# Feed-forwards of an fp32 trunk: the narrow chunk moved to second place, four chunks in seven block products, two of their weight sums by adding DMAs

## The chip, the cores and the metric

One Trainium2 chip, one of its cores. The time is device microseconds of one execution of the whole program, the median of several runs. A page of the profile and a trace come from one more execution, taken by the hardware profiler.

Engines are named as the profile names them: PE is TensorE (matmuls), DVE is VectorE, ACT is ScalarE, POOL is GpSimd, SP is SyncE, which only issues transfers here. Each takes its instructions from a queue of its own, in order.

## What is computed

A trunk of four layers on 256 tokens of width 1024, in fp32. Each layer is a feed-forward, a token mixer (attention) and a second feed-forward; all eight feed-forwards have the same form:

```python
D_FF = 2816
def swiglu(x, w_in, w_out):
    gate, up = jnp.split(x @ w_in, 2, axis=-1)
    return (jax.nn.silu(gate) * up) @ w_out

for i in range(DEPTH):                       # DEPTH = 4
    g = norm_g[i]
    h = h + 0.5 * rms_norm(swiglu(rms_norm(h, g[0]), ffn_w_in[i, 0], ffn_w_out[i, 0]), g[1])
    m = rms_norm(h, g[2])
    ...                                      # one of three kinds of attention
    h = h + rms_norm(m, g[3])
    h = h + 0.5 * rms_norm(swiglu(rms_norm(h, g[4]), ffn_w_in[i, 1], ffn_w_out[i, 1]), g[5])
```

The attention layers are not touched by the change.

## The kernel before

**Precision.** Every fp32 operand of a matmul is split in two float32r parts: ACT casts (`hi`, line 156), DVE subtracts (`lo`, line 157). A product takes three matmuls for each k-tile of 128: hi by hi, lo by hi, hi by lo. The 256 tokens are two token tiles, t = 0 and 1.

**Chunks.** `ffn` (line 283) walks over the 2816 columns of gate and up in six chunks: five of 512 and, last, one of 256. Each chunk computes gate and up for its columns, forms g = silu(gate) * up, transposes g on PE (`turn`, line 425, into `tpg`, then split to `gh` and `gl`) and adds g times its rows of w_out to the banks `y` (`out`, line 436). The w_out part of a chunk follows one chunk later, in units of two k-tiles: two units for a full chunk (k = 0 and 2), one for the narrow one.

**Two forms of a chunk.** `plain` (line 443) multiplies each of gate and up with both token tiles, eight block products of four k-tiles (12 matmuls each) for a full chunk. `wino` (line 466) takes the four quarters of the weights, b00, b01 (gate and up of the first 512 rows), b10, b11 (of the other 512), and makes seven products of sums, in the manner of Winograd and Strassen: b00, b10, t2, t1, t3, b11, t4, in this order, with the first w_out unit of the chunk before behind t2 and the second behind b11. B, A and C are the PSUM banks `pb`, `pa` and `pc`; b00 goes to B alone, ACT copies the bank (line 483, `sl<-pb`), and then t2, t1 and b11 add to the same bank, with a copy by ACT between them. `WINO` names the chunks in this form: 2 and 4.

**Sums of weights.** `plan_wino` (line 358) makes four DVE sums of 128x2048 for a chunk (line 373): b00 += b01, b01 += b11, t2 = b00 + b11, later t2 += b10.

**Buffers and order.** Loads are 1 MB transfers on SP into `raw` buffers, nine of them (`RAWS`). A split unit (hi and lo of 128x2048) lives in one of four buffers (`UNITS`); `fill` (line 398) prepares the next unit of the list as soon as fewer than four are alive. So the split of the fourth unit ahead can start when PE has read the one before it for the last time. The order of each engine's queue is fixed when the program is built, by a scheduler that goes by its own costs. After the last chunk come the rest of the w_out products, `end` (the norm and the new x, in `finish`, line 210) for each token tile, and `turn_x`, which transposes x for the next phase.

Of the kernel before, what the change touches and what calls it, by code (L numbers as in the profile page):

```python
# [16 lines left out]
P = 128  # L17
# [19 lines left out]

RAWS = 9
UNITS = 4
WINO = (2, 4)  # L40

IN_NAMES = ["x", "norm_g", "ffn_w_in", "ffn_w_out", "diff_w_in", "diff_w_out", "diff_lambda",
            "diff_subln", "moba_w_in", "moba_w_out", "nsa_w_in", "nsa_w_out", "nsa_cmp_pe",
# [3 lines left out]
class Trunk:  # L47
# [235 lines left out]
    def ffn(self, l, f, X, ahead, end):  # L283
        nc = self.nc
        with self.tc.tile_pool(name=f"ffn{l}{f}", bufs=2, reuse_waits="tile") as pool:
            w_in, w_out = self.a["ffn_w_in"][l, f], self.a["ffn_w_out"][l, f]
            chunks = [(c, min(512, D_FF - c)) for c in range(0, D_FF, 512)]
            last = len(chunks) - 1
            y = [None, None]
            G, U = {}, {}  # L290
# [32 lines left out]
            def split(n, of, done=False):  # L323
                live["unit"] += 1
                self.n += 1
                nk, w, m = shape.get(of, (4, 512, 4))
                hi = self.wt.tile([P, nk, w], F32R, tag="hi", name=f"hi{self.n}")
                lo = self.wt.tile([P, nk, w], F32R, tag="lo", name=f"lo{self.n}")
                v = R[of][:, :nk * w].rearrange("p (k n) -> p k n", n=w)
                for k in range(0, nk, m):  # L330
                    self.hilo(v[:, k:k + m], hi[:, k:k + m], lo[:, k:k + m])
                if done:
                    free(of)
                U[n] = hi, lo, nk, w

            def close(n):
                U.pop(n)
                live["unit"] -= 1
# [5 lines left out]
            def plan_plain(j):  # L344
                c0, w = chunks[j]
                for b, o in (("g", 0), ("u", D_FF)):
                    if w == 512:
                        for h in range(2):
                            plan((j, b, h), (w_in, h * 512, 4, o + c0, w))
                    else:  # L350
                        plan((j, b, 0), (w_in, 0, 8, o + c0, w))

            def plan_out(j):
                c0, w = chunks[j]
                for k in range(0, w // P, 2):
                    plan((j, "o", k), (w_out, c0 + k * P, 2, 0, D))

            def plan_wino(j):


                c0, w = chunks[j]
                name = lambda n: (j, n)
                quarter = lambda k, u: (w_in, k * 512, 4, u * D_FF + c0, w)
                ko = [(j - 1, "o", k) for k in (0, 2)]
                c1 = chunks[j - 1][0]
                osrc = [(w_out, c1 + k * P, 2, 0, D) for k in (0, 2)]
                for n, src in ((name("b00"), quarter(0, 0)), (name("b01"), quarter(0, 1)),
                               (name("b10"), quarter(1, 0)), (name("b11"), quarter(1, 1)), (name("t2"), None),
                               (ko[0], osrc[0]), (ko[1], osrc[1])):
                    loads.append(lambda n=n, src=src: raw(n, src))  # L370

                def add(to, a, b):
                    nc.vector.tensor_tensor(R[name(to)], R[name(a)], R[name(b)], op=ALU.add)  # L373

                def quarters(n, then=()):
                    split(name(n), name(n))
                    for x in then:
                        add(*x)

                def last_of(n, of, before=None, gone=None):  # L380
                    if before:
                        add(*before)
                    if gone:
                        free(name(gone))
                    split(name(n), name(of), True)

                preps.extend([
                    lambda: quarters("b00", [("b00", "b00", "b01")]),
                    lambda: quarters("b10", [("b01", "b01", "b11"), ("t2", "b00", "b11")]),
                    lambda: split(name("t2"), name("t2")),  # L390
                    lambda: split(ko[0], ko[0], True),
                    lambda: last_of("t1", "b00"),
                    lambda: last_of("t3", "b01"),
                    lambda: last_of("b11", "b11"),
                    lambda: split(ko[1], ko[1], True),
                    lambda: last_of("t4", "t2", ("t2", "t2", "b10"), "b10")])

            def fill():
                while loads and live["raw"] < RAWS:
# [25 lines left out]
            def turn(j, t):  # L425
                n = chunks[j][1] // P
                g = G.pop((j, t))
                tp = self.tp.tile([P, 4, P], F32, tag="mm", name=f"tpg{l}{f}_{j}_{t}")
                for k in range(n):
                    nc.tensor.transpose(tp[:, k, :], g[:, k * P:(k + 1) * P], self.ident)  # L430
                gh = self.gt.tile([P, 4, P], F32R, tag="gh", name=f"gh{l}{f}_{j}_{t}")
                gl = self.gt.tile([P, 4, P], F32R, tag="gl", name=f"gl{l}{f}_{j}_{t}")
                self.hilo(tp[:, :n], gh[:, :n], gl[:, :n])
                G[j, t] = (gh, gl)
# [31 lines left out]
            def wino(j):  # L466
                def times(ps, x, at, n, first):
                    self.product(ps, x, [(at, unit((j, n)))], first, True, more=True)
                    close((j, n))

                def o(t, k):
                    out(j - 1, t, (k,))
                    if t == 1:
                        close((j - 1, "o", k))
                    fill()

                tile = lambda tag, t: pool.tile([P, 512], F32, tag=tag, name=f"{tag}{l}{f}_{j}_{t}")
                add = lambda d, x: nc.vector.tensor_tensor(d, x, d, op=ALU.add)
                s24, s31 = SUMS
                B = bank("pb")  # L480
                times(B, X[0][0], 0, "b00", True)
                sl0 = tile("sl", 0)
                nc.scalar.copy(sl0, B)
                fill()
                turn(j - 1, 0)
                A = bank("pa")
                times(A, X[0][0], 4, "b10", True)
                add(sl0, A)
                nc.scalar.activation(sl0, sl0, AF.Silu, scale=X[0][1])
                fill()  # L490
                turn(j - 1, 1)
                times(B, s24, 0, "t2", False)
                sl1 = tile("sl", 1)
                nc.scalar.copy(sl1, B)
                fill()
                o(0, 0)
                o(1, 0)
                times(B, s31, 4, "t1", False)
                g1 = tile("g", 1)
                nc.scalar.copy(g1, B)  # L500
                fill()
                C = bank("pc")
                times(C, s31, 0, "t3", True)
                add(g1, C)
                fill()
                times(B, s24, 4, "b11", False)
                up(0, B, 512, sl0, j, nr[0])
                fill()
                o(0, 2)
                o(1, 2)  # L510
                times(C, X[1][0], 4, "t4", False)
                add(sl1, C)
                nc.scalar.activation(sl1, sl1, AF.Silu, scale=X[1][1])
                up(1, g1, 512, sl1, j, nr[1], g1)
                fill()
                del G[j - 1, 0], G[j - 1, 1]

            plan_plain(0)
            for j in range(1, last):
                if j in WINO:  # L520
                    plan_wino(j)
                else:
                    plan_plain(j)
                    plan_out(j - 1)
            plan_plain(last)
            plan_out(last - 1)
            plan_out(last)

            SUMS, nr = [], []
# [7 lines left out]

            plain(0, [(0, 0), (1, 0), (0, 1), (1, 1)], [lambda: None, lambda: None, early])
            zig = [(0, 0), (0, 1), (1, 0), (1, 1)]
            for j in range(1, last):  # L540
                if j in WINO:
                    wino(j)
                    continue
                plain(j, zig, [lambda: turn(j - 1, 0), lambda: turn(j - 1, 1)])
                for t in range(NT):
                    out(j - 1, t, (0, 2))
                for k in (0, 2):
                    close((j - 1, "o", k))
                fill()
                del G[j - 1, 0], G[j - 1, 1]  # L550
            plain(last, zig, [lambda: turn(last - 1, 0), lambda: turn(last - 1, 1)])
            out(last - 1, 0, (0, 2))
            turn(last, 0)
            turn(last, 1)
            ahead()
            out(last, 0, (0,))
            turn_x = end(0, y[0])
            out(last - 1, 1, (0, 2))
            for k in (0, 2):
                close((last - 1, "o", k))  # L560
            turn_x()
            out(last, 1, (0,))
            self.later_x = end(1, y[1])

    def turn_x(self):
# [757 lines left out]
```

## Time and profile before

| | |
|---|---|
| median of three runs | 1990.72 us (1990.71 to 1993.12) |
| the profiled execution | 1993.53 us, of it the span 1991.8 us |
| PE, matmul | 1962.8 us busy, 99% of the span, 9904 matmuls |
| DVE | 1481.6 us, 74% |
| ACT | 1153.8 us, 58% |
| POOL | 127.6 us, 6% |
| mean granted TensorE clock | 0.998 of full speed |
| DMA, all 16 engines | 361.51 MB on SP's queue, 52% of their time |

The span runs from the first to the last instruction of the profiled execution; its own time has 1.7 us around that. Matmuls overlap, so their pace is read from starts and not from durations. A share of busy time is a mean over stages that have different limits. The feed-forward that is read most below is the second one, from about 320 to 500 us.

### The profile page before, as it was taken

How to read it: one execution, taken by the hardware profiler on the slowest of the kernel's cores; microseconds unless marked ns; L12 is line 12 of the kernel's file. 1: busy time of each engine (PE TensorE's matmuls, PEld its weight loads, DVE VectorE, ACT ScalarE, POOL GpSimd, SP SyncE). 2: the span in 40 equal slices, each digit the busy share in tenths (PEclk: the TensorE clock that was granted, in tenths of full speed). 3: DMA queues.
4: the chain of work that ended last, by engine and by line, in shares of the span. 5: the costliest groups of instructions: out<-in, count | busy, mean ns of one | idle time of the engine just before them, and what ended most of it. 6: DMA issues, size and time to landing. Idle time of an engine off the chain costs nothing.

```text
span 1991.8 us, 25602 instructions
## 1 busy us (share of the span) xinstructions
PE 1962.8 (99%) x9904; PEld 1625.0 (82%) x9904; DVE 1481.6 (74%) x1944; ACT 1153.8 (58%) x1625; POOL 127.6 (6%) x239
## 2 busy tenths in 40 slices
PE   7999999999999999999999999999999999999998
PEld 6888878888888878888888888678888888878887
DVE  6877677877778666778777777877777877677875
ACT  6555566555555566565554665865466556566553
POOL 0000210000000120000000032000000000210000
PEclk9999999999999999999999999999999999999999
DMA  9543638445664356564646374164538543638540
GB/s 365 209 148 127 207 120 313 170 144 202 230 232 148 106 190 217 185 232 148 222 156 214 129 191 157 64 234 147 211 130 313 192 144 116 206 107 306 191 146 23
DMA packets 168650, 363.14 MB, mean 182 GB/s; under 512 B 7760, under 2 KB 36688, under 8 KB 168528
## 3 DMA queue, kind: packets, MB, share of 16 engines
q1 hardware_dynamic: 168528, 361.51, 52.0%
q8 instruction: 78, 1.28, 0.3%
q14 instruction: 44, 0.36, 0.1%
HBM read 360.43 MB, written 1.05 MB: 181 GB/s over the span
## 4 chain that ended last, share of the span: by engine, by line
PE 92%; DVE 3%; ACT 2%; issue 1%; POOL 0%; DMA 0%; SPq 0%; DVEq 0%; POOLq 0%; ACTq 0%
PE ps L152 31%; PE y L244 9%; PE y L246 9%; PE y L245 9%; PE pb L152 9%; PE pc L152 4%; PE pw L667 4%; PE pw L669 4%; PE pw L668 4%; PE pa L152 2%; PE tpg L430 2%; DVE lo L157 1%; PE sc L741 1%; PE tpx L181 1%; ACT e L752 1%
## 5 line engine op out<-in xcount | busy, mean ns | idle before, releaser
L157 DVE TENSOR_TENSOR lo<-raw,hi 128x2048 fp32r<-128x2048 f32 (+3 forms) x486 | 876.3, 1821 | 313.4 <-ACT hi L156 309.6
L156 ACT CAST hi<-raw 128x2048 fp32r<-128x2048 f32 (+3 forms) x486 | 733.6, 1528 | 508.2 <-PE ps L152 167.3
L152 PE MATMUL ps<-hi,xh 128*128 128x512 f32 (+1 forms) x1024 | 377.7, 369 | 1.8 <-ACT xh L156 1.2
L152 PE MATMUL ps<-hi,xl 128*128 128x512 f32 (+1 forms) x1024 | 372.7, 364 | 0.0
L152 PE MATMUL ps<-lo,xh 128*128 128x512 f32 (+1 forms) x1024 | 372.4, 364 | 0.2 <-DVE lo L157 0.2
L244 PE MATMUL y<-hi,gh 128*128 128x512 f32 x704 | 276.2, 392 | 0.0
L245 PE MATMUL y<-lo,gh 128*128 128x512 f32 x704 | 274.3, 390 | 0.0
L246 PE MATMUL y<-hi,gl 128*128 128x512 f32 x704 | 271.2, 391 | 0.0
L152 PEld LDWEIGHTS ps<-hi,xh 128*128 128x128 f32 x1024 | 193.9, 189 | 31.8 <-ACT xh L156 2.1
L152 PEld LDWEIGHTS ps<-hi,xl 128*128 128x128 f32 x1024 | 193.6, 189 | 31.6 <-DVE xl L157 1.1
L152 PEld LDWEIGHTS ps<-lo,xh 128*128 128x128 f32 x1024 | 194.0, 189 | 30.3 <-DVE lo L157 1.1
L667 PE MATMUL pw<-hi,xh 128*128 128x512 f32 (+2 forms) x432 | 165.3, 383 | 0.0
L246 PEld LDWEIGHTS y<-hi,gl 128*128 128x128 f32 x704 | 131.5, 188 | 32.1 <-DVE gl L157 4.3
L669 PE MATMUL pw<-hi,xl 128*128 128x512 f32 (+2 forms) x432 | 156.4, 362 | 0.0
L668 PE MATMUL pw<-lo,xh 128*128 128x512 f32 (+2 forms) x432 | 156.2, 362 | 0.0
L244 PEld LDWEIGHTS y<-hi,gh 128*128 128x128 f32 x704 | 132.2, 188 | 28.1 <-ACT gh L156 1.7
L245 PEld LDWEIGHTS y<-lo,gh 128*128 128x128 f32 x704 | 132.3, 188 | 26.0
L373 DVE TENSOR_TENSOR raw<-raw,raw 128x2048 f32<-128x2048 f32 x64 | 145.0, 2286 | 0.0
L119 POOL TENSOR_TENSOR st<-st,negh 128x1 f32<-128x1 f32 (+1 forms) x56 | 45.1, 806 | 1491.6 <-DVE st L206 1395.5
L667 PEld LDWEIGHTS pw<-hi,xh 128*128 128x128 f32 x432 | 82.0, 190 | 18.3 <-issue 8.2
L752 ACT ACTIVATE e<-e,st 128x128 f32<-128x128 f32 (+1 forms) x160 | 71.7, 450 | 40.6 <-DVE st L749 39.8
L157 DVE TENSOR_TENSOR gl<-tpg,gh 128x512 fp32r<-128x512 f32 (+1 forms) x96 | 61.0, 642 | 45.6 <-ACT gh L156 45.6
(212 smaller groups left out, 2648.6 us busy)
## 6 DMA issues: line engine op xcount, KB each, us to landing
raw<-in_ffn_w_in SPq DMA_DIRECT2D x172, 1024.0 KB, 7.0
raw<-in_ffn_w_out SPq DMA_DIRECT2D x88, 1024.0 KB, 5.6
raw<-in_diff_w_in SPq DMA_DIRECT2D x24, 1024.0 KB, 5.2
raw<-in_moba_w_in SPq DMA_DIRECT2D x12, 1024.0 KB, 5.3
raw<-in_nsa_w_in SPq DMA_DIRECT2D x9, 1024.0 KB, 5.1
raw<-in_diff_w_out SPq DMA_DIRECT2D x8, 1024.0 KB, 4.9
gpre<-in_norm_g SPq DMA_DIRECT2D x12, 512.0 KB, 5.9
gpost<-in_norm_g SPq DMA_DIRECT2D x12, 512.0 KB, 7.4
```

Source lines behind the costliest of these rows:

```text
L119: self.nc.gpsimd.tensor_tensor(r, v, src, op=ALU.pow)
L152: nc.tensor.matmul(out, l, r, start=first and i == 0, stop=last and i == len(steps) - 1, skip_group_check=more)
L156: self.nc.scalar.copy(hi, src)
L157: self.nc.vector.tensor_tensor(lo, src, hi.bitcast(F32), op=ALU.subtract)
L244: nc.tensor.matmul(y[b], x[0][:, kt, :], hi[:, k, s], start=f, stop=False)
L245: nc.tensor.matmul(y[b], x[0][:, kt, :], lo[:, k, s], start=False, stop=False)
L246: nc.tensor.matmul(y[b], x[1][:, kt, :], hi[:, k, s], start=False, stop=l)
L373: nc.vector.tensor_tensor(R[name(to)], R[name(a)], R[name(b)], op=ALU.add)
L667: nc.tensor.matmul(out, x[0][:, kt, :], hi[:, k, :], start=first and i == 0, stop=False)
L668: nc.tensor.matmul(out, x[0][:, kt, :], lo[:, k, :], start=False, stop=False)
L669: nc.tensor.matmul(out, x[1][:, kt, :], hi[:, k, :], start=False, stop=last and i == len(todo) - 1)
L752: nc.scalar.activation(e[:, c, :], e[:, c, :], AF.Exp, scale=-1.0, bias=top[:, c:c + 1], accum_out=tot[:, c:c + 1])
```

## The change

`WINO` becomes (2, 3, 4, 5). The narrow chunk moves from the end to second place, index 1. So chunk 0 is plain and full, chunk 1 plain and narrow, and chunks 2 to 5 are full chunks in seven products. Of the four big sums in each of them, two stay on DVE (b00 += b01 and t2 = b00 + b11); the two others (b01 += b11 and t2 += b10) are transfers issued by POOL that add to what lies in the destination. The order of sums and splits in the list of units is set anew for it. In the last chunk the second w_out unit of the chunk before comes behind t4, and the products after the last chunk are put in another order. A setting of the build, `dynamic_dma_scratch_size`, goes from 1024 to 2048.

```diff
-WINO = (2, 4)
+WINO = (2, 3, 4, 5)
...
-            chunks = [(c, min(512, D_FF - c)) for c in range(0, D_FF, 512)]
+            chunks = [(c, 512) for c in range(0, D_FF - 256, 512)]
+            chunks.insert(1, (D_FF - 256, 256))
...
-                ko = [(j - 1, "o", k) for k in (0, 2)]
-                c1 = chunks[j - 1][0]
-                osrc = [(w_out, c1 + k * P, 2, 0, D) for k in (0, 2)]
+                c1, w1 = chunks[j - 1]
+                ko = [((j - 1, "o", k), (w_out, c1 + k * P, 2, 0, D)) for k in range(0, w1 // P, 2)]
...
+                def add_by_dma(to, b):
+                    nc.gpsimd.dma_start(R[name(to)], R[name(b)], accum_op=ALU.add)
 
                 def quarters(n, then=()):
                     split(name(n), name(n))
                     for x in then:
-                        add(*x)
-
-                def last_of(n, of, before=None, gone=None):
-                    if before:
-                        add(*before)
+                        (add if len(x) == 3 else add_by_dma)(*x)
+
+                def last_of(n, of, gone=None):
+                    split(name(n), name(of), True)
                     if gone:
                         free(name(gone))
-                    split(name(n), name(of), True)
-
+
+                outs = [lambda n=n: split(n, n, True) for n, _ in ko]
                 preps.extend([
                     lambda: quarters("b00", [("b00", "b00", "b01")]),
-                    lambda: quarters("b10", [("b01", "b01", "b11"), ("t2", "b00", "b11")]),
-                    lambda: split(name("t2"), name("t2")),
-                    lambda: split(ko[0], ko[0], True),
+                    lambda: quarters("b10", [("t2", "b00", "b11"), ("b01", "b11")]),
+                    lambda: quarters("t2", [("t2", "b10")]),
+                    outs[0],
                     lambda: last_of("t1", "b00"),
                     lambda: last_of("t3", "b01"),
-                    lambda: last_of("b11", "b11"),
-                    lambda: split(ko[1], ko[1], True),
-                    lambda: last_of("t4", "t2", ("t2", "t2", "b10"), "b10")])
+                    lambda: last_of("b11", "b11")])
+                if j < last:
+                    preps.extend(outs[1:])
+                preps.append(lambda: last_of("t4", "t2", "b10"))
+                if j == last:
+                    preps.extend(outs[1:])
...
-                o(0, 2)
-                o(1, 2)
+                if j < last and chunks[j - 1][1] == 512:
+                    o(0, 2)
+                    o(1, 2)
...
-            plain(last, zig, [lambda: turn(last - 1, 0), lambda: turn(last - 1, 1)])
-            out(last - 1, 0, (0, 2))
             turn(last, 0)
+            out(last - 1, 0, (2,))
+            ahead()
+            out(last, 0, (0, 2))
             turn(last, 1)
-            ahead()
-            out(last, 0, (0,))
             turn_x = end(0, y[0])
-            out(last - 1, 1, (0, 2))
-            for k in (0, 2):
-                close((last - 1, "o", k))
+            out(last - 1, 1, (2,))
+            close((last - 1, "o", 2))
+            out(last, 1, (0,))
             turn_x()
-            out(last, 1, (0,))
+            out(last, 1, (2,))
```

DVE's queue in the second feed-forward, from the split of b11 in chunk 2 on (`raw387_2965` is its b11, `raw389_2971` its t2; the splits of `raw400_3094` and `raw402_3100` and the next are units of chunk 3, which is plain), before:

```order
L157 TENSOR_TENSOR lo418_3313<-raw387_2965,hi418_3312 128x2048
L373 TENSOR_TENSOR raw389_2971<-raw389_2971,raw380_2861 128x2048
L157 TENSOR_TENSOR lo420_3343<-raw396_3025,hi420_3342 128x2048
L157 TENSOR_TENSOR lo422_3364<-raw389_2971,hi422_3363 128x2048
L478 TENSOR_TENSOR g01_2_1_3360<-pc425_3371,g01_2_1_3360 128x512
L157 TENSOR_TENSOR lo426_3386<-raw400_3094,hi426_3385 128x2048
L422 SCALAR_TENSOR_TENSOR g01_2_0_3403<-pb412_3238,st390_2984,sl01_2_0_3251 128x512
L157 TENSOR_TENSOR lo428_3406<-raw402_3100,hi428_3405 128x2048
L157 TENSOR_TENSOR lo430_3435<-raw411_3236,hi430_3434 128x2048
L478 TENSOR_TENSOR sl01_2_1_3310<-pc425_3371,sl01_2_1_3310 128x512
```

and now DVE's queue from the split of b11 in chunk 3 to t2 of chunk 4 (`raw413_3245` is b11 and `raw416_3266` t2 of chunk 3; `raw421_3320` the second w_out unit; `raw423_3350`, `raw424_3352`, `raw430_3431` and `raw433_3452` are b00, b01, b10 and b11 of chunk 4, `raw436_3482` its t2):

```order
L157 TENSOR_TENSOR lo437_3507<-raw413_3245,hi437_3506 128x2048
L157 TENSOR_TENSOR lo439_3537<-raw421_3320,hi439_3536 128x2048
L482 TENSOR_TENSOR g01_3_1_3554<-pc444_3564,g01_3_1_3554 128x512
L157 TENSOR_TENSOR lo441_3557<-raw416_3266,hi441_3556 128x2048
L157 TENSOR_TENSOR lo445_3579<-raw423_3350,hi445_3578 128x2048
L426 SCALAR_TENSOR_TENSOR g01_3_0_3595<-pb431_3433,st396_3004,sl01_3_0_3446 128x512
L372 TENSOR_TENSOR raw423_3350<-raw423_3350,raw424_3352 128x2048
L157 TENSOR_TENSOR lo446_3598<-raw430_3431,hi446_3597 128x2048
L372 TENSOR_TENSOR raw436_3482<-raw423_3350,raw433_3452 128x2048
L482 TENSOR_TENSOR sl01_3_1_3504<-pc444_3564,sl01_3_1_3504 128x512
L157 TENSOR_TENSOR lo447_3628<-raw436_3482,hi447_3627 128x2048
L426 SCALAR_TENSOR_TENSOR g01_3_1_3554<-g01_3_1_3554,st397_3006,sl01_3_1_3504 128x512
```

The sum of t2 with b10 has left the queue, and the two sums of the next chunk stand between the splits of b00, b10 and t2, ahead of the small sum for `sl` of token tile 1.

ACT's queue at the start of chunk 2 in the second feed-forward (`raw389_2971` is t2, `raw394_3019` the first w_out unit, `pb412` the bank of b00), before:

```order
L156 CAST hi409_3228<-raw389_2971 128x2048
L156 CAST hi410_3232<-raw394_3019 128x2048
L483 COPY sl01_2_0_3251<-pb412_3238 128x512
L156 CAST hi413_3253<-raw376_2845 128x2048
L156 CAST gh01_1_0_3264<-tpg01_1_0_3259 128x512
```

and now at the start of chunk 4 (`raw436_3482` is t2, `raw438_3510` the first w_out unit, `pb450` the bank of b00, `raw423_3350` t1 and `raw424_3352` t3):

```order
L156 CAST hi447_3627<-raw436_3482 128x2048
L518 ACTIVATE sl01_3_1_3504<-sl01_3_1_3504,st368_2826 128x512
L156 CAST hi448_3647<-raw438_3510 128x2048
L487 COPY sl01_4_0_3666<-pb450_3653 128x512
L156 CAST hi451_3668<-raw423_3350 128x2048
L156 CAST gh01_3_0_3679<-tpg01_3_0_3674 128x512
L156 CAST hi454_3698<-raw424_3352 128x2048
L156 CAST gh01_3_1_3708<-tpg01_3_1_3703 128x512
```

The Silu of the chunk before now stands between the cast of t2 and the copy of b00's bank.

## Rows read from the trace of the kernel before

**Rows 1.** The page's first part: busy us, share of the span and count by engine.
```profile
PE 1962.8 (99%) x9904; PEld 1625.0 (82%) x9904; DVE 1481.6 (74%) x1944; ACT 1153.8 (58%) x1625; POOL 127.6 (6%) x239
```

**Rows 2.** PE's waits over the whole span, longest in total first.
```profile
engine line waited for: us in total, times, longest us
PE tpx L181 <- DVE xg L173: 8.2, 1, 8.2
PE tpf L698 <- DVE on L969: 4.0, 4, 1.2
...
PE ps L152 <- ACT xh L156: 1.2, 1, 1.2
```

**Rows 3.** PE's instructions in order: start us, duration us, engine, line, operation.
```profile
167.77 0.28 PE L152 MATMUL ps<-hi,xl 128*128 128x256 f32 x1
167.89 0.28 PE L152 MATMUL ps<-hi,xh 128*128 128x256 f32 x1
...
371.03 0.39 PE L152 MATMUL pb<-hi,xh 128*128 128x512 f32 x1
371.25 0.39 PE L152 MATMUL pb<-lo,xh 128*128 128x512 f32 x1
...
377.29 0.47 PE L152 MATMUL pb<-hi,sh 128*128 128x512 f32 x1
...
388.37 0.39 PE L152 MATMUL pc<-hi,sh 128*128 128x512 f32 x1
```

**Rows 4.** Busy time of each engine in a block-product chunk and in a feed-forward.
```profile
core 0: us, PE busy (x) PEld busy (x) DVE busy (x) ACT busy (x) POOL busy (x), PEclk, DMA share, GB/s
371.02:401.95 30.93, 30.93 (x141) 25.42 (x140) 26.12 (x17) 21.83 (x16) 0.00 (x0) 1.00 0.76 273
323.00:490.00 167.00, 167.00 (x807) 139.76 (x806) 124.98 (x93) 89.59 (x80) 1.08 (x2) 1.00 0.52 186
```

**Rows 5.** DVE's instructions around chunk 2 of the second feed-forward, columns as in 3.
```profile
366.84 4.49 DVE L373 TENSOR_TENSOR raw<-raw,raw 128x2048 f32<-128x2048 f32 x2
373.38 6.70 DVE L157 TENSOR_TENSOR lo<-raw,hi 128x2048 fp32r<-128x2048 f32 x3 [2.05 <-ACT hi L156]
379.99 0.69 DVE L157 TENSOR_TENSOR gl<-tpg,gh 128x512 fp32r<-128x512 f32 x1
...
393.20 0.68 DVE L478 TENSOR_TENSOR g<-pc,g 128x512 f32<-128x512 f32 x1
393.80 2.28 DVE L157 TENSOR_TENSOR lo<-raw,hi 128x2048 fp32r<-128x2048 f32 x1
396.00 0.74 DVE L422 SCALAR_TENSOR_TENSOR g<-pb,st,sl 128x512 f32<-128x512 f32 x1
396.66 2.28 DVE L157 TENSOR_TENSOR lo<-raw,hi 128x2048 fp32r<-128x2048 f32 x1
```

**Rows 6.** ACT's instructions in the same feed-forward, columns as in 3.
```profile
332.27 0.69 ACT L416 ACTIVATE sl<-ps,st 128x512 f32<-128x512 f32 x1
332.86 1.90 ACT L156 CAST hi<-raw 128x2048 fp32r<-128x2048 f32 x1
...
371.44 3.71 ACT L156 CAST hi<-raw 128x2048 fp32r<-128x2048 f32 x2 [9.18 <-DVE raw L373]
375.06 0.57 ACT L483 COPY sl<-pb 128x512 f32<-128x512 f32 x1
375.53 1.91 ACT L156 CAST hi<-raw 128x2048 fp32r<-128x2048 f32 x1
377.35 0.58 ACT L156 CAST gh<-tpg 128x512 fp32r<-128x512 f32 x1
377.82 1.92 ACT L156 CAST hi<-raw 128x2048 fp32r<-128x2048 f32 x1
...
388.57 0.59 ACT L500 COPY g<-pb 128x512 f32<-128x512 f32 x1 [0.31 <-PE pb L152]
```

**Rows 7.** DMA issues: tensor, queue, count, KB each, median us to landing.
```profile
raw<-in_ffn_w_in SPq DMA_DIRECT2D x172, 1024.0 KB, 7.0
...
out<-h SPq DMA_DIRECT2D x4, 256.0 KB, 2.0
```

More of the change, by code (lines that the diff above doesn't have):

```diff
@@ L363, in plan_wino @@
                 quarter = lambda k, u: (w_in, k * 512, 4, u * D_FF + c0, w)
-                ko = [(j - 1, "o", k) for k in (0, 2)]
-                c1 = chunks[j - 1][0]
-                osrc = [(w_out, c1 + k * P, 2, 0, D) for k in (0, 2)]
+                c1, w1 = chunks[j - 1]
+                ko = [((j - 1, "o", k), (w_out, c1 + k * P, 2, 0, D)) for k in range(0, w1 // P, 2)]
                 for n, src in ((name("b00"), quarter(0, 0)), (name("b01"), quarter(0, 1)),
-                               (name("b10"), quarter(1, 0)), (name("b11"), quarter(1, 1)), (name("t2"), None),
-                               (ko[0], osrc[0]), (ko[1], osrc[1])):
+                               (name("b10"), quarter(1, 0)), (name("b11"), quarter(1, 1)), (name("t2"), None), *ko):
                     loads.append(lambda n=n, src=src: raw(n, src))
@@ L515, in wino @@
                 fill()
-                del G[j - 1, 0], G[j - 1, 1]
+                if j < last:
+                    del G[j - 1, 0], G[j - 1, 1]
             plan_plain(0)
-            for j in range(1, last):
+            for j in range(1, last + 1):
                 if j in WINO:
@@ L524, in ffn @@
                     plan_out(j - 1)
-            plan_plain(last)
-            plan_out(last - 1)
             plan_out(last)
@@ L539, in ffn @@
             zig = [(0, 0), (0, 1), (1, 0), (1, 1)]
-            for j in range(1, last):
+            for j in range(1, last + 1):
                 if j in WINO:
@@ L1311 @@
     nc = bacc.Bacc("TRN2", target_bir_lowering=False, num_devices=1,
-                   dynamic_dma_scratch_size=1024)
+                   dynamic_dma_scratch_size=2048)
     arrays, args = {}, {}
```

## Prediction

> **What bounds the kernel now.** I read the page first, then PE's list of waits, then one block-product chunk of the second feed-forward. PE is busy for 99% of the span [rows 1] and its list of waits [rows 2] is all but empty: the largest entry is the start, 8.2 us, the next ones belong to attention (tpf, sc, tph: 4.0 us or less in all), the first products of a phase (ps) follow with 1.2, and no bank of a block-product chunk (pa, pb, pc) stands in it. So the bound is PE's count of instructions. The pace is read from starts, since the durations overlap: a 512-column matmul every 0.227 us (371.03 to 371.25), a 256-column one every 0.12 us [rows 3]. A plain full chunk has 96 input matmuls, a block-product chunk 7 x 12 = 84. The granted clock is 1.00 in all windows read [rows 4].
>
> The second thing to see is how near the next engine is. In the chunk from 371.02 to 401.95 us PE works 30.93 us, DVE 26.12 and ACT 21.83 [rows 4]. That chunk follows a plain one and is followed by a plain one, which take DVE fewer splits, and PE never waits. The question is what four such chunks in a row do.
>
> **The removed work.** Two more chunks of each of eight feed-forwards use seven products: 2 x 8 x 12 = 192 matmuls fewer, 192 x 0.2267 = **43.5 us** less PE time. The narrow chunk and the products with w_out keep their counts and only move.
>
> **The added work.** A split is an ACT cast and a DVE subtraction; from one start to the next they take 1.81 and 2.20 us (371.44 and 375.06; 373.38 and 379.99) [rows 5, 6]. A block-product chunk needs seven splits instead of four, so DVE gets 2 x 3 x 2.2 = 13.2 us more in each feed-forward. Its big sums stay at eight: two in each of four chunks, instead of four in two, the other two by DMA. In a run of such chunks DVE has in each 9 splits, 2 sums (11 x 2.2), two gl (1.2), three small sums (1.8) and two products with the gate (1.3): 28.5 us against PE's 30.9. On average it fits. The chain does not, as the queues' order shows.
>
> **The chain of a third or fourth block chunk.** Let 0 be the start of its b00 product. PE before it: t4 from -2.72, the second w_out unit from -8.16, b11 from -10.88, t3 from -13.60. The first w_out unit ends five matmuls before t3, at -14.7. Only four split units may live, so the split of the second one starts then: ACT sees PE's end 0.2 us later (388.37 to 388.57) [rows 3, 6], casts for 1.91, and DVE begins at -12.6. From there DVE works through its queue without a hole: lo 2.2, small sum 0.6, lo of t4 2.2, lo of b00 2.2, gate product 0.66, sum b00+b01 2.2, lo of b10 2.2, and the sum for t2, which ends at +1.95. ACT's queue then has, in this order, the cast for t2 (1.81, from 2.05), a Silu (0.6, by 332.27 to 332.86), the cast of a w_out unit (1.81) and the copy of b00's bank (0.57) [rows 6]. The copy ends near 6.9. PE may not add t2 into that bank sooner, and it got there at 2.72 + 0.36 (transposes) + 2.8 = 5.9: **it waits 1.1 us**. In the chunk of before this sum ends at 371.33, 0.3 after b00's start (371.03), the copy at 375.63, and t2 starts at 377.29: 1.7 us to spare [rows 3, 5, 6].
>
> A second wait follows in the same chunk. Behind the copy ACT casts t1, gh of token tile 0, t3, and then gh of tile 1: 0.47 for the copy, 1.81, 0.47, 1.81 and 0.58 for the last [rows 6], from the copy's start at 6.3 to 11.4, some 4.6 us after t2's start. PE wants it one product, one turn and four matmuls after that, at 4.0: **0.6 us** more. Round the loop, from one t2 to the next, this makes 32.4 us for 30.9, 1.5 lost.
>
> **The second block chunk** comes behind the first, which has one w_out unit instead of two, since the narrow chunk has two k-tiles: PE has 5.44 us less to do while DVE saves only 2.2. From t1's end (-8.16): +0.2, a copy 0.47, the cast of b00 1.91, so DVE's lo of b00 runs from -5.5; then 2.2 + 0.6 + 2.2 + 2.2 + 2.2 and a gate product of 0.75, done at +4.6. PE's transposes of that very g stand behind b00, at 2.72: 1.95 us late. The copy, as above, ends at 8.9 and t2 could start at 7.85: 1.1 more. Together **3.1 us**.
>
> **The first** follows the narrow chunk: PE has 12.2 us of products and 10.9 of w_out there while DVE has four splits; its t2 sum ends some 4 us before b00 starts. Nothing lost. **The end** of a feed-forward: the chain from the last y to the transposed x has five DVE steps, now with one gl (0.6) among them; PE has 22 matmuls (5.0 us) before it needs x, as before, and now a turn (0.36) too. Before it had no wait there [rows 2]. I take 0; were the cover gone it would be under 1 us at each of seven ends between a feed-forward and what follows it.
>
> Sum for one feed-forward: 3.1 + 1.5 + 1.5 + 0.6 (the second wait of the last chunk) = 6.7 us, eight times 53.6 us.
>
> **The adding DMAs.** Two in each block chunk, 64 in all, on POOL's queue, which has 1.08 us of work in the 167 us of a feed-forward [rows 4]; behind them stand only the pow of the norm at its end. The first (b01 += b11) starts when DVE has read b01, at -2.45 in the chain above, and ACT's cast of t3 wants it at 9.1: a window of 11.5 us. The second (t2 += b10) has 13.9. No row shows such a transfer. Below, a small store lands in 2.0 us; above, three loads one after the other, 3 x 7.0 = 21 [rows 7]. Loads ran at 273 GB/s with a DMA share of 0.76 [rows 4], so 1 MB fills all engines for 2.9 us, and a load's landing has 4.1 on top. An add reads two megabytes; I take 2 x 2.9 + 4.1 = 9.9 us, nearest to a load, inside both windows: nothing. Each microsecond past a window holds ACT's queue, with the gh cast and the next chunk's casts behind it, and costs 3 x 8 = 24 us; at 21 it would be over 200. DVE is not slowed by fewer sums; a gain beyond the sums already taken from its queue is excluded.
>
> The Trainium skill ("DMA: Bandwidth & Descriptors", section on the anatomy of one DMA, SWDGE path) gives a GpSimd transfer about 2.0 us plus its bytes at 436 GB/s; by that, an estimate, such an add takes 4.4 us and the windows are wide. The rows for loads here (7.0) are slower than that. The same page ("Issuing engines are not separate DMA queues") says that transfers from all queues share the same 16 engines, which speaks against the change; no run here shows it yet.
>
> **The sum.** The profiled execution took 1993.53 us (span 1991.8), 2.8 above the median of 1990.72. 1993.5 - 43.5 + 53.6 = 2003.6, less 2.8: **2001 us**.
>
> **The rivals.**
> 1. The waits do not bite, faster: 1990.7 - 43.5 = 1947 with none of them, 1972 if only the second chunk's 3.1 us are paid (24.8). For it: the loop is 32.4 us of which I need only 1.5 less, 5%, and every hand-over is read to 0.1 us at best; PE shows no such wait today [rows 2]. Against: the steps are back to back in fixed queues, with durations that repeat to 1%.
> 2. The DMA engines become the bound, slower still. Six loads fill them 17.5 us of a chunk's 32.4, which leaves 7.4 for each add. If an add costs three passes (read, read, write), 8.8 us, the chunk takes 35.1: 2.7 x 3 x 8 = 65 us more, 2066. It decides from 7.4 us of engine time or 11.5 us to landing. For it: share 0.76 in today's chunk [rows 4]. Against: the mean over a feed-forward is 0.52.
> 3. The waits and the gain cancel: 6.7 comes out as 5.4, 1991. That the products are not removed is no rival: PE's queue is shorter by just 192.
>
> **How the numbers follow.** Forecast (1995 to 2015) 0.46; rival 2 or late adds (2015 and up) 0.23; rival 3, within 0.2% (which is about what a measurement of this kernel can tell from no change) 0.12; rival 1 0.19, of it 0.06 below 1972. So slower 0.69, same 0.12, faster 0.19. The range goes from 1972 to 2066; about 0.06 lies below and 0.10 above. The forecast's own range is 1995 to 2015.
>
> **What would show it.** PE busy near 1920 us and a list of waits that is no longer empty: tpg and pb on ACT's sl copy or DVE's g, about 2.0 us once and 1.1 us three times in each feed-forward, y on ACT's gh, 0.6 us. DVE idle shrinks in chunks three to five. Adds that land within 11 us, with no ACT cast waiting for a DMA, would confirm the cover. It is wrong if PE's waits sum to far less than 50 us, or if casts wait for the adds.

## The result, and the profile after

The changed kernel takes **2005.25 us** (median of 4 runs, 2003.10 to 2006.29) against 1991.90 of the kernel before on the same chip: ratio 1.0065, 95% interval 1.0052 to 1.0077. It is slower, by about what was forecast (2001 us, 1995 to 2015). The profiled execution took 2004.23 us with a span of 2002.3, which is 10.5 more than before, at the same mean granted clock (0.998). Since 43.5 us of products are gone, 54.0 us of PE's time went into something new (by the medians 13.4 + 43.5 = 56.9).

The page of the changed kernel, its busy times (1), the queue of the adding transfers (3: packets, MB, share of the engines), chain (4) and two of its DMA issues (6):

```profile
span 2002.3 us, 25733 instructions
PE 1932.5 (97%) x9712; PEld 1584.9 (79%) x9712; DVE 1609.4 (80%) x2040; ACT 1257.2 (63%) x1721; POOL 188.6 (9%) x303
q0 software_dynamic: 9216, 67.11, 17.6%
PE 79%; ACT 8%; DVE 7%; issue 3%; POOL 0%; ACTq 0%; DVEq 0%; POOLq 0%
...
raw<-in_ffn_w_in SPq DMA_DIRECT2D x172, 1024.0 KB, 8.4
raw<-raw POOLq DMA_DIRECT2D x64, 1024.0 KB, 7.0
```

PE has 192 instructions fewer than in [rows 1], and is now 97% busy instead of 99%. In the chain that ended last PE has 79%, where it had 92% before; ACT and DVE have grown from 5% to 15%. PE's list of waits (engine and line, tile, what it waited for: us in total, times, longest), which was empty of block chunks in [rows 2]:

```profile
PE pb L152 <- ACT sl L487: 21.1, 24, 0.9
PE tpg L434 <- DVE g L426: 14.1, 8, 1.8
...
PE y L244 <- ACT gh L156: 5.1, 24, 0.2
```

All three are new, with just the counts of the forecast: the copy of b00's bank 24 times (three block chunks in each of eight feed-forwards), g 8 times (the second block chunk), gh 24 times. They add up to 40.3 us. A recorded wait begins at the modelled end of the matmul before it, 0.39 us behind its start, while the next one would have started 0.227 behind it; so each wait is 0.17 us longer than recorded, and 56 of them make 9.5 us more. Together that is 49.8 of the 54.0; the remaining 4.2 are not placed.

PE in the second feed-forward of the changed kernel, at the three kinds of wait (start, duration, ..., idle before and what ended it):

```profile
389.40 0.39 PE L152 MATMUL pb<-hi,xl 128*128 128x512 f32 x1
391.55 0.66 PE L434 MATMUL tpg<-ident,g 128*128 128x128 f32 x4 [1.76 <-DVE g L426]
394.59 0.39 PE L152 MATMUL pa<-hi,xl 128*128 128x512 f32 x1
395.80 0.50 PE L152 MATMUL pb<-hi,sh 128*128 128x512 f32 x1 [0.83 <-ACT sl L487]
400.38 0.50 PE L244 MATMUL y<-hi,gh 128*128 128x512 f32 x1 [0.21 <-ACT gh L156]
424.10 0.60 PE L434 MATMUL tpg<-ident,g 128*128 128x128 f32 x4
428.34 0.51 PE L152 MATMUL pb<-hi,sh 128*128 128x512 f32 x1 [0.90 <-ACT sl L487]
456.68 0.60 PE L434 MATMUL tpg<-ident,g 128*128 128x128 f32 x4
```

The first transposes of a chunk (tpg) mark its loop: 391.55 to 424.10 is 32.55 us, 424.10 to 456.68 is 32.58, for 30.93 in [rows 4]. And the chain that PE waits for, DVE's part and ACT's, in the third block chunk (b00 starts at 421.37):

```profile
421.10 2.28 DVE L372 TENSOR_TENSOR raw<-raw,raw 128x2048 f32<-128x2048 f32 x1
...
425.42 2.29 DVE L157 TENSOR_TENSOR lo<-raw,hi 128x2048 fp32r<-128x2048 f32 x1 [1.44 <-ACT hi L156]
```

```profile
423.49 1.90 ACT L156 CAST hi<-raw 128x2048 fp32r<-128x2048 f32 x1 [8.16 <-DVE raw L372]
425.30 0.72 ACT L518 ACTIVATE sl<-sl,st 128x512 f32<-128x512 f32 x1
425.92 1.89 ACT L156 CAST hi<-raw 128x2048 fp32r<-128x2048 f32 x1
427.71 0.57 ACT L487 COPY sl<-pb 128x512 f32<-128x512 f32 x1
```

ACT sits idle for 8.16 us until DVE's sum for t2 ends at 423.4, then does cast, Silu, the cast of the w_out unit and the copy in a row; PE starts t2 as the copy ends. In [rows 3, 5] the same sum ended 0.3 us behind b00's start, here 2.0.

### The profile page after: what moved, and what is told of

The parts are those of the page before. It is cut to its first block, busy times and chain, and to the rows that moved or that the text cites. A ratio compares the mean times of both kernels' runs of the same rounds, so it can differ in the third digit from the quotient of the medians.

```text
span 2002.3 us, 25733 instructions
## 1 busy us (share of the span) xinstructions
PE 1932.5 (97%) x9712; PEld 1584.9 (79%) x9712; DVE 1609.4 (80%) x2040; ACT 1257.2 (63%) x1721; POOL 188.6 (9%) x303
## 3 DMA queue, kind: packets, MB, share of 16 engines
q0 software_dynamic: 9216, 67.11, 17.6%
## 4 chain that ended last, share of the span: by engine, by line
PE 79%; ACT 8%; DVE 7%; issue 3%; POOL 0%; ACTq 0%; DVEq 0%; POOLq 0%
PE ps L152 13%; PE pb L152 12%; PE y L246 9%; PE y L244 9%; PE y L245 9%; PE pc L152 6%; ACT hi L156 5%; PE pa L152 4%; PE pw L670 4%; PE pw L672 4%; PE pw L671 3%; DVE lo L157 3%; DVE raw L372 2%; PE tpg L434 1%; ACT gh L156 1%
## 5 line engine op out<-in xcount | busy, mean ns | idle before, releaser
L157 DVE TENSOR_TENSOR lo<-raw,hi 128x2048 fp32r<-128x2048 f32 (+3 forms) x534 | 984.7, 1861 | 251.3 <-ACT hi L156 250.8
L156 ACT CAST hi<-raw 128x2048 fp32r<-128x2048 f32 (+3 forms) x534 | 824.8, 1563 | 481.6 <-DVE raw L372 189.9
L152 PE MATMUL ps<-hi,xh 128*128 128x256 f32 (+1 forms) x512 | 175.4, 342 | 1.9 <-ACT xh L156 1.3
L152 PE MATMUL pb<-hi,sh 128*128 128x512 f32 x384 | 153.1, 399 | 21.1 <-ACT sl L487 21.1
L152 PE MATMUL ps<-lo,xh 128*128 128x256 f32 (+1 forms) x512 | 173.2, 338 | 0.2 <-DVE lo L157 0.2
L152 PE MATMUL ps<-hi,xl 128*128 128x256 f32 (+1 forms) x512 | 172.9, 338 | 0.0
L152 PE MATMUL pb<-lo,sh 128*128 128x512 f32 x384 | 151.8, 395 | 0.0
L152 PE MATMUL pb<-hi,sl 128*128 128x512 f32 x384 | 149.5, 389 | 0.0
L152 PEld LDWEIGHTS ps<-hi,xh 128*128 128x128 f32 x512 | 97.6, 191 | 13.2 <-ACT xh L156 2.2
L152 PEld LDWEIGHTS ps<-lo,xh 128*128 128x128 f32 x512 | 97.6, 191 | 11.2 <-DVE lo L157 1.1
```

Of the source, the lines that this page charges most:

```text
L152: nc.tensor.matmul(out, l, r, start=first and i == 0, stop=last and i == len(steps) - 1, skip_group_check=more)
L156: self.nc.scalar.copy(hi, src)
L157: self.nc.vector.tensor_tensor(lo, src, hi.bitcast(F32), op=ALU.subtract)
```

## The experiments

Theory A is the forecast's: latency of that one chain through fixed queues, with the adding transfers hidden. B: the transfers cost the time. C: DVE or ACT has too much to do in block chunks. All were timed beside the kernel before, whose medians lie between 1990.89 and 1991.44 us there, and the ratios are to it. Edits are to the changed kernel where nothing else is said; the kernels of the first two experiments and of the second one under "The w_out unit ahead of t2" leave sums out and so compute something else.

### One DVE sum less

```diff
-                    lambda: quarters("b00", [("b00", "b00", "b01")]),
+                    lambda: quarters("b00"),
```

> The changed kernel without one of the two sums that DVE makes in each block-product chunk (b00 += b01 is left out; 32 sums of 2.2 us in all). Theory A, the prediction's chain (the sum for t2 ends 1.95 us behind the start of b00, ACT's copy of the bank stands behind it): all of the chain comes 2.2 us earlier, so the copy (late by 1.1), the transposes of the second block chunk (late by 1.95) and the gh cast (late by 0.6) are in time but for some 0.8 us once a feed-forward. PE's waits on the copy and on g fall from 35.2 us recorded to under 8, the loop of a third or fourth block chunk from 32.6 to 30.9 us, the time from 2005 to 1950 to 1965. Theory B, the adding transfers fill the DMA engines or hold up casts: they are all still there, time 1998 to 2006.

Measured: 1954.99 us, ratio 0.9814 (0.9798 to 0.9830). PE's waits on the copy, on gh and on g are gone from its list; the new entry, and two starts a loop apart:

```profile
PE pb L152 <- DVE lo L157: 4.8, 8, 1.2
...
415.95 0.60 PE L434 MATMUL tpg<-ident,g 128*128 128x128 f32 x4
446.85 0.60 PE L434 MATMUL tpg<-ident,g 128*128 128x128 f32 x4
```

The loop is 30.90 us, and the span (1953.5) is 5.2 above 1991.8 - 43.5 = 1948.3. So the products are saved in full, and 2.2 us of one chain decide over 50 us. B falls: all 64 transfers are still there. So are the moved narrow chunk, the new end and the larger `dynamic_dma_scratch_size`, which leaves them some 5 us at most. C is not excluded by this run, since DVE has less to do.

### No adding transfers

```diff
-                    lambda: quarters("b10", [("t2", "b00", "b11"), ("b01", "b11")]),
-                    lambda: quarters("t2", [("t2", "b10")]),
+                    lambda: quarters("b10", [("t2", "b00", "b11")]),
+                    lambda: quarters("t2"),
```

> The changed kernel without its 64 adding transfers (b01 += b11 and t2 += b10 are left out). Theory A, the transfers land in their windows and cost nothing: 2002 to 2007, the same waits of PE on ACT's copy and on g as in the changed kernel (35.2 us recorded). Theory B, their 5.5 us of all DMA engines each slow the loads, or a cast waits for them: faster by 10 us or more, to 1995 or below. What DVE does is unchanged.

Measured: 2004.30 us, ratio 1.0063 (1.0048 to 1.0078), as with them. The waits are the same to 0.1 us:

```profile
PE pb L152 <- ACT sl L487: 21.0, 24, 0.9
PE tpg L434 <- DVE g L426: 14.0, 8, 1.8
```

So the transfers are hidden, and B is out.

### The two sums back on DVE

```diff
-                    lambda: quarters("b10", [("t2", "b00", "b11"), ("b01", "b11")]),
-                    lambda: quarters("t2", [("t2", "b10")]),
+                    lambda: quarters("b10", [("t2", "b00", "b11"), ("b01", "b01", "b11")]),
+                    lambda: quarters("t2", [("t2", "t2", "b10")]),
```

> The changed kernel with its two adding transfers made by DVE instead (b01 += b11 behind the sum for t2, t2 += b10 behind the difference of t2). DVE gets 2 x 2.2 us more in each block chunk, 32.9 us of work in a loop that takes 32.6. Theory A, with the adds hidden in the changed kernel: the loop grows by 2 to 4.4 us, the time to 2050 to 2120. Theory B (the transfers cost about what the sums would): 1995 to 2015.

Measured: 2040.13 us, ratio 1.0239 (1.0224 to 1.0254): slower by 34.9 us than with the transfers, short of the 45 that were the least expected. PE waits 29.3 us for g (14.1 with the transfers), and the loop, read at the last two of these starts, is 33.56 us, 1.0 more instead of 2 to 4.4:

```profile
PE tpg L434 <- DVE g L426: 29.3, 9, 4.0
...
398.98 1.11 PE L434 MATMUL tpg<-ident,g 128*128 128x128 f32 x4 [3.96 <-DVE g L426]
431.65 0.60 PE L434 MATMUL tpg<-ident,g 128*128 128x128 f32 x4
465.21 0.60 PE L434 MATMUL tpg<-ident,g 128*128 128x128 f32 x4
```

Two sums of 2.2 us more make a loop 1.0 longer: part of them goes into gaps that DVE has while it waits for ACT (1.44 us at 425.42 above is one). DVE is now busy for 33.12 of the 33.56 us. So the transfers do save time against sums on DVE, by less than theory A said and by more than B. Part of the 34.9 us is the clock, which no theory had: in or just behind each of seven waits for g of about 4.0 us the granted clock falls to the lower of its two levels (1.2 of 2.4 GHz) for a while, as at 398.98, where four transposes take 1.11 us instead of 0.60. The mean granted clock is 0.991 instead of 0.998, by an estimate from these two figures up to some 14 us of PE's time in 2038.7.

### The copy first

Same instructions, other queues. `issue_after(x)` puts what its block issues behind x in the queue of x's engine; besides, the split of the first w_out unit is issued no longer at the end of the chunk before, and `unit` fills only if its unit is missing.

```diff
-                nc.scalar.copy(sl0, B)
-                fill()
-                turn(j - 1, 0)
+                cp = nc.scalar.copy(sl0, B).ins
+                with self.tc.issue_after(cp):
+                    ga, gd = turn(j - 1, 0)
+                with self.tc.issue_after(ga), self.tc.issue_after(gd):
+                    if live["unit"] < UNITS:
+                        preps.pop(0)()
...
-                fill()
-                turn(j - 1, 1)
                 times(B, s24, 0, "t2", False)
+                ga, gd = turn(j - 1, 1)
+                with self.tc.issue_after(ga), self.tc.issue_after(gd):
+                    fill()
```

> The changed kernel, same instructions, other order of the queues in a block-product chunk: ACT copies b00's bank before it casts the w_out unit, gh of token tile 0 comes right behind the copy, gh of tile 1 (whose transposes now come behind t2) ahead of the casts of t1 and t3. Theory A (the latency of one chain through fixed queues): in the third and fourth block chunk the copy ends near 4.5 us behind b00's start where PE wants it at 5.9, so the loop falls to 30.9 to 31.3 us; the transposes of the second block chunk, which wait for g, are still 1.9 us late. 1965 to 1985. Theory C (DVE or ACT have too much work in a row of block chunks, whatever the order): the loop stays at 32.0 to 32.6, the time at 1998 to 2006. Theory B (DMA): 1998 to 2006 as well.

Measured: 1978.45 us, ratio 0.9936 (0.9921 to 0.9950), faster than both. ACT in the third block chunk, PE's waits, and the loop:

```profile
418.81 1.91 ACT L156 CAST hi<-raw 128x2048 fp32r<-128x2048 f32 x1 [8.36 <-DVE raw L372]
...
421.24 0.56 ACT L489 COPY sl<-pb 128x512 f32<-128x512 f32 x1
421.70 0.59 ACT L156 CAST gh<-tpg 128x512 fp32r<-128x512 f32 x1
...
PE tpg L435 <- DVE g L427: 14.1, 8, 1.8
PE pb L152 <- DVE lo L157: 5.1, 16, 0.4
...
419.22 0.60 PE L435 MATMUL tpg<-ident,g 128*128 128x128 f32 x4
450.72 0.60 PE L435 MATMUL tpg<-ident,g 128*128 128x128 f32 x4
```

With not an instruction less, the wait on the copy is gone (21.1 us before) and the one on gh too, and the loop is 31.50, a little over the 30.9 to 31.3 expected. That rules C out as the cause of 32.6. The order of several things changed together here, so the gain isn't split between the copy and the other moves. The wait for g in the second block chunk is untouched, to the tenth.

### The w_out unit ahead of t2

```diff
+                o(0, 0)
+                o(1, 0)
                 times(B, s24, 0, "t2", False)
                 sl1 = tile("sl", 1)
                 nc.scalar.copy(sl1, B)
                 fill()
-                o(0, 0)
-                o(1, 0)
```

with the split of t2, and DVE's sum for it, behind that unit's split in `preps`, and the order inside the chunk held by `issue_after`.

> The changed kernel, same instructions, with the first w_out unit of the chunk before placed ahead of the product t2 instead of behind it, on PE and in the list of splits; the DVE sum for t2 comes behind that unit's split, the g product of tile 1 ahead of the small sum of the next chunk. PE then wants t2 at 11.6 us behind b00's start instead of 6.2, which covers the chain of sum, cast and difference (8 to 10 us) and leaves the copy of b00's bank 8 us. Theory A: hardly a wait of PE left in the block chunks (under 10 us in all), loop 30.9, 1948 to 1965. Theory C (DVE's or ACT's amount of work): loop 32.0 or more, 1995 to 2010. Theory B (DMA): 1995 to 2010.

Measured: 2015.79 us, ratio 1.0120 (1.0105 to 1.0135): all three theories missed, A by over 50 us. ACT's waits, which have no such entry in the changed kernel, and one of them:

```profile
ACT hi L156 <- DMA raw<-raw: 47.1, 19, 3.9
...
380.44 1.91 ACT L156 CAST hi<-raw 128x2048 fp32r<-128x2048 f32 x1 [2.59 <-DMA raw<-raw]
```

t2 += b10 can't start before DVE has read t2 for its lo. That came later here, so POOL issued the transfer at 372.17 and t4's cast waited until 380.44, with a copy of PE's bank behind it in ACT's queue. The next run takes this transfer out:

```diff
-                        quarters("t2", [("t2", "b10")])
+                        quarters("t2")
```

> out_first without its second adding transfer (t2 += b10 is left out). out_first came out at 2016 where 1948 to 1965 was expected; its ACT waits 47 us for adding transfers, which are issued later there, behind the later difference of t2, and wanted by t4's cast at the same time as before. If this late transfer is what it lost by: 1980 to 1998, and no wait of ACT on a transfer of that line. If the loss is DVE's order (the sum for t2 ahead of the g product of tile 1, the g product of tile 0 behind a sum and a difference): 2008 to 2016.

Measured: 1981.84 us, ratio 0.9950 (0.9933 to 0.9966). ACT's wait on a transfer is gone, and so is PE's wait for g (23.7 us with it). 34 us of out_first's loss were this transfer, out of its cover. The rest, 31 us above 1948.3 by the spans, isn't placed one by one; PE's largest entry in the block chunks there, of three between 4 and 5.4 us, is this:

```profile
PE pb L152 <- ACT hi L156: 5.4, 8, 0.7
```

### Three block chunks, none in a row

```diff
-WINO = (2, 3, 4, 5)
+WINO = (1, 3, 5)
-            chunks.insert(1, (D_FF - 256, 256))
+            chunks.insert(2, (D_FF - 256, 256))
```

> Three block chunks instead of four, none behind another: order full, block, narrow, block, full, block, with the adding transfers as in the changed kernel. 8 x 12 matmuls fewer than before, 21.8 us. Theory A (the waits come from block chunks in a row): hardly a wait of PE, 1966 to 1976. Theory C (each block chunk costs DVE and ACT time that PE pays, in a row or not): three quarters of the 54 us, 1995 to 2012.

Measured: 1992.71 us, ratio 1.0002 (0.9992 to 1.0011): neither A's 1966 to 1976 nor quite C. PE's waits, the first feed-forward on PE, DVE and ACT, and two windows there (PE, PEld, DVE, ACT and POOL busy, granted clock, DMA share, GB/s):

```profile
PE y L244 <- ACT hi L156: 8.4, 8, 1.1
PE pb L152 <- ACT hi L156: 5.5, 1, 5.5
...
50.90 0.80 PE L152 MATMUL pb<-hi,sh 128*128 128x512 f32 x1 [5.53 <-ACT hi L156]
52.70 1.22 PE L244 MATMUL y<-hi,gh 128*128 128x512 f32 x2 [1.00 <-ACT hi L156]
...
46.03 0.69 DVE L157 TENSOR_TENSOR gl<-tpg,gh 128x512 fp32r<-128x512 f32 x1 [0.36 <-ACT gh L156]
46.63 2.28 DVE L372 TENSOR_TENSOR raw<-raw,raw 128x2048 f32<-128x2048 f32 x1
...
48.95 7.31 ACT L156 CAST hi<-raw 128x2048 fp32r<-128x2048 f32 x4 [2.34 <-DVE raw L372]
...
48.00:52.00 4.00, 0.80 (x1) 0.29 (x1) 2.04 (x2) 3.05 (x2) 0.00 (x0) 0.55 0.02 4
52.00:56.00 4.00, 3.30 (x8) 2.62 (x9) 4.00 (x3) 4.00 (x3) 0.87 (x1) 0.50 0.32 66
```

Of waits on the copy, gh or g there is none, so block chunks apart pay nothing of that kind. What they pay is new and stands in the block chunk right behind chunk 0: 1.1 us in each feed-forward for the cast of the w_out unit (8.4 us, with 0.17 each 9.8), and once, at the start of the program, 5.5 us for the cast of t2, whose DVE sum stands behind the gl of tile 1 and starts only at 46.63; then PE goes on at the lower of the clock's two levels (1.2 of 2.4 GHz; granted 0.55 and 0.50). Its loads are not the reason: the four loads of this chunk's weights had landed by 30.3 us. DVE does the sum straight behind that gl, so it is the order of its queue that puts it so late. The 1.1 us have to do with an order too: in these eight chunks PE's queue has two w_out matmuls behind the first matmul of t2 (52.70 behind 50.90) and ahead of the eleven others, while in the sixteen other block chunks all twelve come first, and none of those waits. From 40 to 60 us PE gets 49 matmuls done where the kernel before does 94: 45 x 0.227 = 10.2 us. 9.8 and 10.2 make the 20 by which the span (1989.8) stands above 1991.8 - 21.8 = 1970; the first feed-forward's wait for the cast, 1.2 us, is in both.

### The narrow chunk back at the end

copy_first with `WINO = (1, 2, 3, 4)`, the narrow chunk last, and the end of a feed-forward as before.

> The order of copy_first, and the narrow chunk back at the end as in the kernel before: chunks 1 to 4 in seven products, then the narrow one, with the end of a feed-forward as before. No block chunk follows one that has a single w_out unit. Theory A: the 1.9 us that PE still waited for g in the second block chunk (14.1 us recorded in copy_first) go, what is left is the loop of 31.5 for 30.9 three times in each feed-forward: 1955 to 1968. Theory D (it is the second block chunk in a row as such, not the missing w_out unit, that is late): the wait stays, 1973 to 1982.

Measured: 1979.57 us, ratio 0.9935 (0.9920 to 0.9950), no better than copy_first, and over A's range by 12; the time alone would fit D. But the wait for g, 14.1 us, is gone from the list, so D falls: it comes from the missing w_out unit. In its place stand the two waits of the run before:

```profile
PE y L244 <- ACT hi L156: 7.0, 8, 1.0
PE pb L152 <- ACT hi L156: 5.5, 1, 5.5
```

### The lo of t2 last, and both places mixed

In `product`, for t2 alone, with `late` set by its call:

```diff
+        if late:
+            steps = [s for i, s in enumerate(steps) if i % 3 != 1] + steps[1::3]
```

> copy_first, with the twelve matmuls of product t2 in another order: the eight that read hi first, the four that read lo last, so that lo is wanted 8 x 0.227 = 1.8 us later. Theory A (what is left in the loop, 31.5 for 30.9, is PE's wait for the lo of t2, 5.1 us recorded in 16 waits): those waits go, loop 30.9 to 31.1, 1968 to 1974. If the loop is held by something else: 1977 to 1980.

Measured: 1975.59 us, ratio 0.9920 (0.9903 to 0.9936). The 5.1 us on lo are gone from PE's list, and 4.3 on gh have come back:

```profile
PE y L246 <- ACT gh L158: 4.3, 16, 0.3
```

The time is 2.9 us lower than copy_first instead of 4.5 to 10.5, and the two intervals overlap, so the gain is barely shown. What is next in the chain takes over.

> The order of copy_first_lo_late, the narrow chunk second in the very first feed-forward (where a block chunk in second place waited 5.5 us for its loads, with the clock at 0.83 in that stretch) and last in the seven others. Theory A: against narrow_last_copy_first (1979.6) the start gives 9 to 12 us back and the lo of t2 about 8, so 1955 to 1966; left are the 0.9 to 1.0 us that the first block chunk of each of the seven waits for the cast of its w_out unit. If the wait at the start is paid in another place: 1966 to 1976.

The 5.5 us were no wait for loads, as said above.

Measured: 1969.23 us, ratio 0.9883 (0.9868 to 0.9898), the fastest here, 21.7 us under the kernel before and 36.0 under the changed one. That is 3 us above A's range and inside the other one, though not for the reason given there. Both early waits and seven of the eight on g are gone, gh stays:

```profile
PE y L246 <- ACT gh L158: 5.1, 21, 0.3
PE tpg L439 <- DVE g L431: 1.8, 1, 1.8
...
342.56 0.70 PE L246 MATMUL y<-hi,gh 128*128 128x512 f32 x2
343.10 1.08 PE L154 MATMUL pb<-lo,sh 128*128 128x512 f32 x4
```

The wait for the w_out unit's cast, which was to stay in the seven feed-forwards with a block chunk in second place, is gone there as well. With lo last, eight matmuls of t2 stand ahead of the two w_out matmuls in PE's queue instead of one (the last two lines, from the second feed-forward), and that covers the cast. So it was PE's order and not the place of the chunk. The span, 1967.5, is still 19 us above 1948.3; the waits on gh, with 0.17 each, are 8.7 of them, and the rest isn't placed.

## Why the prediction was right, step by step

- **The bound and the removed work** (43.5 us): right. With one sum less PE comes to within 5.2 us of it.
- **The second block chunk** (1.95 + 1.1 us): 1.92 us for the transposes (391.55, where the last matmul before them, at 389.40, makes 389.63), and 0.98 for t2 (0.83 recorded; 395.80, where the last matmul before it, at 394.59, makes 394.82). Right, and copy_first and narrow_last_copy_first show that the first belongs to the missing w_out unit.
- **The loop** (32.4 us): 32.54 and 32.59 from one t2 to the next (395.80, 428.34, 460.93). The terms behind it: the copy 1.1, measured 1.06 (428.34 is 4.24 behind the transposes at 424.10, where these and the twelve matmuls of b10 take 3.18); gh 0.6, measured 0.2 recorded, 0.4 with the 0.17. DVE has a little more to do than counted, 29.4 us in a loop and not 28.5 (windows at the end).
- **The sum**: 2.9 + 1.6 + 1.7 + 0.4 = 6.6 us in a feed-forward where 6.7 was forecast, 52.8 in eight for 53.6; by the spans 54.0. First block chunk and end without a wait: right. That the sum agrees to 0.1 us is partly luck, since its terms miss by up to 0.2 in both directions and the medians give 56.9.
- **The adding transfers**: hidden, as forecast, but by a size that was wrong. I took 9.9 us to landing; they take 7.0 (6.9 to 9.7). In engine time 17.6% of 2002.3 us over 64 is 5.5 us each, I took 5.8. The figure that the Trainium skill gives ("DMA: Bandwidth & Descriptors", section on the anatomy of one DMA) led to an estimate of 4.4 us. The trace, with 7.0, doesn't agree. That a late add holds ACT's queue, which the working named as its price, is what out_first shows.
- **What would show it**: PE busy "near 1920" came out at 1932.5. The step forgot that a matmul ahead of a wait counts with its modelled 0.39 us instead of 0.227; some 56 such waits make most of the difference.
- **The rivals**: rival 1 (waits that do not bite) was the price of 2.2 us in DVE's queue or of ACT's order, as one_sum_less and copy_first show; rival 2 is excluded by no_adds, and for rival 3 the waits came out too large.

My theory failed outside the forecast, where I moved things: in out_first I left out that t2's later difference moves the transfer behind it, and in three_spread and narrow_last_copy_first that the order in which PE, and DVE at the start, do things in the block chunk right behind chunk 0 makes waits of its own. In adds_on_dve I took all of DVE's added work for a longer loop.

## What to carry to other kernels

When a queue is busy 90% of a loop, as DVE's was here, read the latency of its longest chain, hand-over by hand-over, against the moment at which the bound engine wants its end: here seven waits of 0.4 to 1.9 us in each feed-forward ate the whole gain of the dropped matmuls. Before work is dropped, try the order of the queues: a copy that frees the bound engine's bank belongs ahead of casts that are wanted later, and this, with the other moves of copy_first, was worth 27 us without an instruction less. A transfer that is hidden now stays so only while nothing moves its start; count its issue among what a reordered step drags along.

## What had not been expected of the hardware

- Adding transfers lengthen the loads beside them without costing the kernel anything here: a 1 MB load of w_in lands in 8.4 us (median) with them and in 5.5 without, one of w_out in 9.2 and 5.5; the DMA share of a loop goes from 0.57 to 0.85. The Trainium skill ("DMA: Bandwidth & Descriptors", section "Issuing engines are not separate DMA queues") says that all queues share the engines, and these rows agree.

```profile
390.90:423.50 32.60, 30.91 (x138) 25.06 (x139) 29.43 (x20) 20.22 (x17) 1.71 (x2) 1.00 0.85 258
```

```profile
390.90:423.50 32.60, 30.49 (x136) 24.68 (x137) 29.41 (x20) 20.21 (x16) 0.00 (x0) 1.00 0.57 195
```

The first is the window of the changed kernel, the second that without the transfers; ahead of the GB/s stands the DMA share.

- While PE did nothing for 5.5 us in three_spread, the granted clock fell, and it stood near 0.5 for some 8 us of work after that (0.55, 0.50): a single wait at the start cost about twice its length. The clock fell with each wait of about 4.0 us in adds_on_dve too.
